# First token block and first weights in halves on two queues, the first weights split in columns, nine warming products

## The chip, the cores and the metric

The kernel runs on one core of one Trainium2 chip. A core has TensorE (PE in the profile, its weight loads PEld), VectorE (DVE), ScalarE (ACT), GpSimd (POOL) and SyncE (SP), and 16 DMA engines that all its queues share. The metric is the device time of one execution in microseconds (us), the median of three runs.

## The reference, cut to what matters

One layer of a hybrid decoder in float32 for 256 prompt tokens and 8 decode tokens, one step each:

```python
x = x + 0.5 * swiglu(rmsnorm(x, n1), f1g, f1u, f1d)      # D_MODEL 2048, D_FF 5504
h = rmsnorm(x, nm)
proj = h @ w_in                                          # q, k, v | RWKV-7 columns
o_att, k_buf, v_buf = attend(q, k, v, sinks)             # window 128, cached K and V for the decode tokens
o_rwkv, shift, S = rwkv_time_mix(proj[..., ATT_COLS:], shift0, wkv0, ...)
x = x + concatenate([o_att, o_rwkv], -1) @ w_out
x = x + 0.5 * swiglu(rmsnorm(x, n2), f2g, f2u, f2d)
```

A final RMSNorm follows, and the new caches and states are outputs too. The time goes into the weight products: 2048 x 5504 matrices, three in each feed-forward part, w_in and w_out.

## The kernel before

The 264 tokens are kept transposed: 16 blocks of 128 features (`KD`) by 264 tokens (`T`). Weights stream from memory in chunks of 128 x 512 float32, 256 KB (`chunk`, L128 to L138): SyncE issues the DMA into `raw` (six buffers), ScalarE casts it to `hi` (L137), and VectorE computes `lo` = raw − hi (`tt`, L64; four buffers of each). The activations are split into high and low parts in the same way. `gemm` (L140 to L155) then makes three matmuls for each 128 x 128 block: hi with the high part, hi with the low part, lo with the high part (all recorded at L80), and adds them up in a bank of PSUM.

`first_ffn` (L302) opens the kernel. `x0` holds the gains of the norm and the first token block, 128 x 280 or 140 KB; ScalarE's queue loads it (L318). `load(0)` splits the block: the high part on ScalarE (L74), the low part on VectorE (L67). The first weight chunk is made ahead of the rest, x1 comes over ScalarE's queue and x2, x3 over SyncE's (L326), the other twelve blocks in groups of four over ScalarE's (L331). Meanwhile TensorE runs `NWARM` products of a tile of ones with itself, which nothing reads.

The mixing stage holds projections, RWKV chunks, attention and w_out at once. Its pieces are generator tasks that are spawned and advanced between weight chunks; the order in which each engine gets its instructions is then set by a list scheduler that simulates the whole program with costs of its own. So an edit at the head can move instructions far behind it. Four things of this stage are spoken of below:

- `m<-kr,bk` on TensorE: products of one RWKV chunk, masked on VectorE into `gm`. SyncE gathers `gm` into `sa` (L520) and loads it back as `X` and `Xt` (L579, L581).
- `dec_scores` (L832): loads the cached keys, `kc`, four times for each half of the heads, 128 KB each, through `load` (L371, ring `ld` of six buffers). Two loads feed the first group of products `m<-qb,ld`, two the second. kc1 to kc4 are those of the second call.
- `dec_attend` (L850): loads `bd`, then `cv`, for the softmax and the values of the decode tokens.
- L946: sixteen reloads of the residual blocks, `x<-xsp`, 132 KB each, over SyncE.

SyncE issues its DMAs strictly in order, so the place in its list decides when a load starts.

Of the kernel before, what the change touches and what calls it, by code (L numbers as in the profile page):

```python
# [7 lines left out]
F32 = mybir.dt.float32  # L8
F32R = mybir.dt.float32r
AF = mybir.ActivationFunctionType  # L10
ALU = mybir.AluOpType
AX = mybir.AxisListType

P = 128
# [10 lines left out]
HALF = (slice(0, 64), slice(64, 128))  # L25
PARTS = [8, 7, 7, 7, 7, 7]
BATCH = [2, 2, 2, 2]
CH, NRAW, NHL = 4, 6, 4
NACC, NM = 3, 5
NH, NQ, NT, NLD = 16, 8, 16, 6  # L30
ROW = 320
NWARM = 11
NGM, NKR, NUV, NTT, NBT = 10, 5, 3, 2, 5
LAG = (11, 7, 7, 7)
P1 = 1
# [17 lines left out]
def body(tc, I, O):  # L53
    nc = tc.nc
    V, A, G, TE, SP = nc.vector, nc.scalar, nc.gpsimd, nc.tensor, nc.sync
# [3 lines left out]
    def uid(s):  # L59
        cnt[0] += 1  # L60
        return f"{s}{cnt[0]}"

    def tt(e, out, a, b, op):
        return e.tensor_tensor(out=out, in0=a, in1=b, op=op)  # L64
# [14 lines left out]
    def mm(out, lhsT, rhs, start=True, stop=True, **k):  # L79
        return TE.matmul(out, lhsT, rhs, start=start, stop=stop, **k)  # L80
# [24 lines left out]
    with ExitStack() as ctx:  # L105
        cp = ctx.enter_context(tc.tile_pool(name="cp", bufs=1))
        sp = ctx.enter_context(tc.tile_pool(name="sp", bufs=1))
        wp = ctx.enter_context(tc.tile_pool(name="wp", bufs=1))
# [8 lines left out]
        def pairs(*rows):  # L117
            return [(t[j], t[j - 1]) for t in rows for j in range(len(t) - 1, 0, -2)]
# [8 lines left out]
        def mp():  # L127
            return pp.tile([P, 512], F32, tag="m", bufs=NM, name=uid("m"))  # L128

        def chunk(src, n, e, ahead=True):  # L130
            w = n * P
            with tc.high_priority() if ahead else nullcontext():
                raw = wp.tile([P, CH * P], F32, tag="raw", bufs=NRAW, name=uid("raw"))
                hi = wp.tile([P, CH * P], F32R, tag="hi", bufs=NHL, name=uid("hi"))
                lo = wp.tile([P, CH * P], F32R, tag="lo", bufs=NHL, name=uid("lo"))
                SP.dma_start(raw[:, :w], src)
                A.copy(hi[:, :w], raw[:, :w])  # L137
                tt(e, lo[:, :w], raw[:, :w], hi[:, :w].bitcast(F32), ALU.subtract)  # L138
            return hi, lo
# [27 lines left out]
        warm = mp()  # L167
        for _ in range(NWARM):
            mm(warm[:, :P], ones, ones)
# [136 lines left out]
        def first_ffn(n2):  # L306
            def load(k0):
                return n1.split(xr[k0], True)

            def nxt(o):  # L310
                n2.split(xr[o])
                n2.square(xr[o])
                A.dma_start(xsp[o], xr[o])

            with tc.tile_pool(name="f1", bufs=1) as fp:
                cur[0] = (fp, NH)
                x0 = fp.tile([P, KD + T], F32, name="x0")
                A.dma_start(x0, I["x0"])  # L318
                n1 = Norm(VG1, pairs(*xs4), ob, gains=x0[:, 0:KD])
                xr = [x0[:, KD:]]  # L320
                at = load(0)
                with tc.issue_after(at.ins):
                    first = chunk(I["gu1"][0, 0][:, 0:CH * P], CH, V, False)
                for e, j0, j1 in ((A, 1, 2), (SP, 2, 4)):
                    xg = fp.tile([P, j1 - j0, T], F32, name=uid("x"))
                    e.dma_start(xg, I["xT"][:, j0:j1, :])  # L326
                    xr += [xg[:, j] for j in range(j1 - j0)]

                def more(q):
                    xg = fp.tile([P, 4, T], F32, tag="x", bufs=3, name=uid("x"))  # L330
                    tc.keep_in_program_order(A.dma_start(xg, I["xT"][:, q * 4:q * 4 + 4, :]))  # L331
                    xr.extend(xg[:, j] for j in range(4))

                ffn(n1, xr, I["gu1"], I["dn1"], nxt, load, more, None, first)
# [703 lines left out]
        kvb, ob, yb = blk("kv", 6), blk("o", 8), blk("y", 8)  # L1038
        n2, n3 = Norm(VGM, pairs(*xs4), ob), Norm(VG2)
        first_ffn(n2)  # L1040
        with tc.tile_pool(name="dx", bufs=1) as dx:
            XD = dx.tile([P, 8, NPAIR, NB], F32, name="XD")
# [103 lines left out]
```

## Time and profile before

| | |
|---|---|
| median of three runs | 1949.77 us (1949.31, 1949.77, 1951.75) |
| profiled execution | 1950.27 us |
| its span | 1948.5 us (1.77 us lie around it) |
| granted TensorE clock, mean | 0.997 |
| TensorE busy | 1934.1 us, 99% of the span |
| DMA, mean | 184 GB/s |

"L80 PE MATMUL acc<-x,hi" in a row is line, engine, operation, and the tiles written and read with their numbers left out. SPq and ACTq rows are DMA issues on SyncE's and ScalarE's queues: a start, and how long the issues of the row took together. A figure in square brackets is the engine's idle time just before, with what ended it. A float32 product of small tiles makes two records of one matmul.

### The profile page before, as it was taken

The page shows a single profiled execution, that of the slowest core. Times are in us where ns is not written, and L with a number is a line of the kernel's source. Part 1 is how long each engine was busy: PE and PEld are TensorE (multiplying, and loading weights), DVE is VectorE, ACT ScalarE, POOL GpSimd, SP SyncE. Part 2 cuts the span into 40 slices and gives each one's busy share as a digit, 9 for nine tenths or more (in the row PEclk, how much of TensorE's full clock was granted, in tenths as well). Part 3 has the DMA queues.
Part 4 walks back from the last instruction along what each step waited for, and adds up shares of the span by engine and source line. Part 5 has one row for each costly group of instructions (what it writes and reads, how often), then busy time and mean ns, then how long its engine had stood idle before and what let it go on. Part 6 is the DMA issues. An engine that isn't in the chain of part 4 may idle for free.

```text
span 1948.5 us, 45522 instructions
## 1 busy us (share of the span) xinstructions
PE 1934.1 (99%) x17131; PEld 1917.4 (98%) x17131; DVE 1307.8 (67%) x2591; ACT 1035.9 (53%) x2069; POOL 260.6 (13%) x382
## 2 busy tenths in 40 slices
PE   9999999999999999999999999999999999999998
PEld 9999999999999999999899999999999999999998
DVE  5865555655556567799867877866666666666665
ACT  5644444444444456666477645644444444444445
POOL 0401102010010112231102100210101001010012
PEclk9999999999999999999999999999999999999999
DMA  7666666665656567565545656566666666666664
GB/s 240 179 194 193 186 194 195 185 189 179 188 182 184 184 193 233 162 173 155 146 133 151 200 157 183 176 187 188 192 191 193 187 193 190 193 194 184 195 181 149
DMA packets 220958, 358.10 MB, mean 184 GB/s; under 512 B 34866, under 2 KB 74434, under 8 KB 220738
## 3 DMA queue, kind: packets, MB, share of 16 engines
q1 hardware_dynamic: 214226, 346.59, 59.6%
q10 hardware_dynamic: 6512, 8.61, 1.3%
q8 instruction: 134, 2.20, 0.4%
q14 instruction: 86, 0.70, 0.1%
HBM read 347.48 MB, written 9.70 MB: 183 GB/s over the span
## 4 chain that ended last, share of the span: by engine, by line
PE 98%; DMA 1%; DVE 1%; ACT 0%; issue 0%; SPq 0%; DVEq 0%; ACTq 0%
PE acc L80 89%; PE m L80 8%; DMA x<-in_x 0%; DMA t<-dr 0%; DVE y L64 0%; DMA ld<-in_cv 0%; PE m L535 0%; DVE lo L64 0%; SPq L581 0%; DMA ld<-in_bias 0%; ACT t L74 0%; PE m L493 0%; PE m L528 0%; PE m L812 0%; ACT hi L137 0%
## 5 line engine op out<-in xcount | busy, mean ns | idle before, releaser
L64 DVE TENSOR_TENSOR lo<-raw,hi 128x512 fp32r<-128x512 f32 (+1 forms) x1288 | 875.6, 683 | 522.8 <-ACT hi L137 499.4
L137 ACT CAST hi<-raw 128x512 fp32r<-128x512 f32 (+1 forms) x1288 | 776.8, 606 | 803.3 <-PE acc L80 724.5
L80 PE MATMUL acc<-x,hi 128*128 128x264 f32 x4840 | 900.2, 287 | 1.5 <-DVE st L64 1.3
L80 PEld LDWEIGHTS acc<-x,hi 128*128 128x128 f32 x4840 | 753.3, 189 | 5.0 <-ACT t L74 1.5
L80 PE MATMUL acc<-x,lo 128*128 128x264 f32 x2420 | 692.8, 286 | 0.0
L80 PE MATMUL acc<-h,hi 128*128 128x264 f32 x2752 | 495.0, 284 | 0.0
L80 PEld LDWEIGHTS acc<-x,lo 128*128 128x128 f32 x2420 | 458.3, 189 | 1.5 <-DVE lo L64 0.4
L80 PEld LDWEIGHTS acc<-h,hi 128*128 128x128 f32 x2752 | 424.4, 189 | 0.0
L80 PE MATMUL acc<-h,lo 128*128 128x264 f32 x1376 | 387.8, 284 | 0.0
L80 PEld LDWEIGHTS acc<-h,lo 128*128 128x128 f32 x1376 | 259.2, 189 | 0.0
L64 POOL TENSOR_TENSOR t<-t,t 128x264 f32<-128x264 f32 x74 | 79.8, 1078 | 1095.6 <-DVE t L64 958.2
L80 PE MATMUL acc<-y,hi 128*128 128x264 f32 x648 | 122.7, 284 | 0.0
L80 PE MATMUL acc<-o,hi 128*128 128x264 f32 x648 | 120.1, 284 | 0.0
L80 PE MATMUL acc<-kv,hi 128*128 128x264 f32 x582 | 109.7, 284 | 0.0
L80 PEld LDWEIGHTS acc<-y,hi 128*128 128x128 f32 x648 | 101.2, 189 | 0.1
L80 PEld LDWEIGHTS acc<-o,hi 128*128 128x128 f32 x648 | 100.1, 189 | 0.0
L67 DVE SCALAR_TENSOR_TENSOR x<-acc,x 128x264 f32<-128x264 f32 x192 | 81.2, 427 | 24.5 <-PE acc L80 23.6
L80 PE MATMUL acc<-y,lo 128*128 128x264 f32 x324 | 92.0, 284 | 0.0
L80 PE MATMUL acc<-o,lo 128*128 128x264 f32 x324 | 92.0, 284 | 0.0
L80 PEld LDWEIGHTS acc<-kv,hi 128*128 128x128 f32 x582 | 90.2, 189 | 0.1
L64 DVE TENSOR_TENSOR t<-acc,t 128x264 f32<-128x264 f32 x156 | 67.4, 432 | 32.8 <-PE acc L80 32.7
L80 PE MATMUL acc<-kv,lo 128*128 128x264 f32 x291 | 82.9, 285 | 0.0
(300 smaller groups left out, 1637.5 us busy)
## 6 DMA issues: line engine op xcount, KB each, us to landing
raw<-in_gu SPq DMA_DIRECT2D x688, 256.0 KB, 3.3
raw<-in_dn SPq DMA_DIRECT2D x224, 256.0 KB, 2.9
raw<-in_win SPq DMA_DIRECT2D x152, 256.0 KB, 3.5
raw<-in_dn SPq DMA_DIRECT2D x160, 192.0 KB, 2.8
raw<-in_wout SPq DMA_DIRECT2D x64, 256.0 KB, 3.5
xsp<-x ACTq DMA_DIRECT2D x16, 132.0 KB, 3.7
x<-xsp SPq DMA_DIRECT2D x16, 132.0 KB, 4.0
ld<-in_sT SPq DMA_DIRECT2D x16, 128.0 KB, 4.4
```

The lines of the kernel that those rows point to most:

```text
L64: return e.tensor_tensor(out=out, in0=a, in1=b, op=op)
L67: return V.scalar_tensor_tensor(out=out, in0=a, scalar=s, in1=b, op0=op0, op1=op1)
L80: return TE.matmul(out, lhsT, rhs, start=start, stop=stop, **k)
L137: A.copy(hi[:, :w], raw[:, :w])
```

## The change

`NWARM` goes from 11 to 9. `x0` and the first weight chunk are each loaded as two halves of 64 partitions, the first 64 by SyncE and the last 64 by ScalarE, x0 first. The DMAs of x1 and of x2, x3 are issued next, and the split of the first block is ordered behind x1's DMA. The cast of the first chunk and its subtraction are each made in two pieces, columns 0 to 127 and 128 to 511, kept in program order behind that split. What is computed stays the same. Lines behind the edit are numbered 10 higher.

```diff
-NWARM = 11
+NWARM = 9
...
-                A.dma_start(x0, I["x0"])
+                raw = wp.tile([P, CH * P], F32, tag="raw", bufs=NRAW, name=uid("raw"))
+                hi, lo = (wp.tile([P, CH * P], F32R, tag=t, bufs=NHL, name=uid(t)) for t in ("hi", "lo"))
+                for d, src in ((x0, I["x0"]), (raw, I["gu1"][0, 0][:, 0:CH * P])):
+                    for e, r in zip((SP, A), HALF):
+                        e.dma_start(d[r], src[r])
                 n1 = Norm(VG1, pairs(*xs4), ob, gains=x0[:, 0:KD])
                 xr = [x0[:, KD:]]
-                at = load(0)
-                with tc.issue_after(at.ins):
-                    first = chunk(I["gu1"][0, 0][:, 0:CH * P], CH, V, False)
                 for e, j0, j1 in ((A, 1, 2), (SP, 2, 4)):
                     xg = fp.tile([P, j1 - j0, T], F32, name=uid("x"))
-                    e.dma_start(xg, I["xT"][:, j0:j1, :])
+                    ins = e.dma_start(xg, I["xT"][:, j0:j1, :])
+                    if e is A:
+                        at = ins
                     xr += [xg[:, j] for j in range(j1 - j0)]
+                with tc.issue_after(at.ins):
+                    at = load(0)
+                with tc.issue_after(at.ins):
+                    for c in (slice(0, P), slice(P, CH * P)):
+                        tc.keep_in_program_order(A.copy(hi[:, c], raw[:, c]))
+                        tc.keep_in_program_order(tt(V, lo[:, c], raw[:, c], hi[:, c].bitcast(F32), ALU.subtract))
+                first = hi, lo
```

The order of the instructions at three places. First ScalarE at the head, before (x_116 is x0, raw_120 the first chunk, x_126 is x1):

```order
L318 DMA x_116<-in_x 128x280
L74 ACT_TABLE_LOAD
L74 ACTIVATE eps<-eps 128x1
L326 DMA x_126<-in_xT 128x264
L74 ACTIVATE x_106<-x_116 128x264
L137 CAST hi_121<-raw_120 128x512
L74 ACTIVATE x_106<-x_126,x_116 128x264
```

and after (x_114 is x0, raw_115 the first chunk, x_122 is x1):

```order
L322 DMA x_114<-in_x 64x280
L74 ACT_TABLE_LOAD
L74 ACTIVATE eps<-eps 128x1
L322 DMA raw_115<-in_gu 64x512
L327 DMA x_122<-in_xT 128x264
L74 ACTIVATE x_104<-x_114 128x264
L335 CAST hi_116<-raw_115 128x128
L335 CAST hi_116<-raw_115 128x384
L74 ACTIVATE x_104<-x_122,x_114 128x264
```

ScalarE's queue has one more DMA, ahead of x1, and the cast is in two pieces; SyncE has the other two halves ahead of x2 and x3.

Second SyncE in the mixing stage, from the third pair of bias loads on, before (ld_16027, ld_16031, ld_16082 and ld_16086 are kc1 to kc4; x_15848 takes the first eight reloads):

```order
L371 DMA ld_15920<-in_bias 128x256
L136 DMA raw_16137<-in_wout 128x512
L371 DMA ld_16027<-in_kc 128x256
L371 DMA ld_16031<-in_kc 128x256
L136 DMA raw_16184<-in_wout 128x512
L136 DMA raw_16213<-in_wout 128x512
L371 DMA ld_16082<-in_kc 128x256
L371 DMA ld_16086<-in_kc 128x256
L946 DMA x_15848<-xsp_90 128x264
```

and after (ld_16084 and ld_16088 are kc3 and kc4; kc1 and kc2 stand first and third behind the bias pair, and left out are kc2, the fourteen reloads ahead of the last two, and two weight chunks):

```order
L381 DMA ld_15922<-in_bias 128x256
L381 DMA ld_16029<-in_kc 128x256
L136 DMA raw_16215<-in_wout 128x512
...
L956 DMA x_15851<-xsp_102 128x264
L956 DMA x_15851<-xsp_103 128x264
L381 DMA ld_16084<-in_kc 128x256
L136 DMA raw_16319<-in_wout 128x512
L381 DMA ld_16088<-in_kc 128x256
L136 DMA raw_16347<-in_wout 128x512
L136 DMA raw_16381<-in_wout 128x512
L381 DMA ld_16168<-in_bd 128x129
```

kc3 and kc4 stood ahead of all sixteen reloads and now stand behind them; the weight chunks stand two places earlier among their own kind.

Third TensorE where it reads them, before (qb_10434 holds the queries of the decode tokens):

```order
L80 MATMUL m_16026<-qb_10434,ld_16031 128x2x4 x2
L80 MATMUL acc_16036<-x_106,hi_16038 128x264 x2
...
L80 MATMUL acc_16036<-x_106,lo_16039 128x264
L812 MATMUL m_16070<-C,t_15546 128x128
...
L814 MATMUL m_16076<-C,t_15547 128x128
L80 MATMUL m_16026<-qb_10434,ld_16082 128x2x4 x2
L80 MATMUL m_16026<-qb_10434,ld_16086 128x2x4 x2
L80 MATMUL acc_16091<-x_106,hi_16093 128x264 x2
```

and after:

```order
L80 MATMUL m_16028<-qb_10436,ld_16033 128x2x4 x2
L80 MATMUL acc_16038<-x_104,hi_16040 128x264
...
L824 MATMUL m_16072<-C,t_15547 128x128
L80 MATMUL m_16028<-qb_10436,ld_16084 128x2x4
L822 MATMUL m_16078<-C,t_15550 128x128
L823 MATMUL m_16078<-C,t_15549 128x128
L824 MATMUL m_16078<-C,t_15549 128x128
L80 MATMUL m_16028<-qb_10436,ld_16084 128x2x4
L80 MATMUL m_16028<-qb_10436,ld_16088 128x2x4 x2
L80 MATMUL acc_16093<-x_104,hi_16095 128x264 x2
```

Counted from the start of TensorE's matmuls with the warming products left out, kc4's first product is number 8979 in both programs, and one product of kc3 has moved ahead of three transposes. The last product `m<-kr,bk` ahead of it is number 8758 before and 8780 after.

## The prediction

> **What bounds the kernel now.** I read the share of each engine first, then the shares of the chain that ended last, then TensorE's waits.
>
> ```profile
> PE 1934.1 (99%) x17131; PEld 1917.4 (98%) x17131; DVE 1307.8 (67%) x2591; ACT 1035.9 (53%) x2069; POOL 260.6 (13%) x382
> PE 98%; DMA 1%; DVE 1%; ACT 0%; issue 0%; SPq 0%; DVEq 0%; ACTq 0%
> ```
>
> TensorE is busy for 99% of the span and holds 98% of the chain. Work on another engine counts only where it makes TensorE wait, or lets its clock fall. The waits that matter here, by what ended them (total, times, longest):
>
> ```profile
> PE m L80 <- issue: 1.7, 1, 1.7
> PE acc L80 <- DVE st L64: 1.3, 1, 1.3
> PE acc L80 <- ACT hi L137: 0.3, 1, 0.3
> PE m L80 <- DMA ld<-in_cv: 0.3, 1, 0.3
> ```
>
> The one wait that the edited code touches is the third, 0.3 us at the head. The others lie in the mixing stage, whose order also moves. The head first: one row of the chain (start, length), the others of the timeline.
>
> ```profile
> 0.73 4.49 DMA x<-in_x
> ```
>
> ```profile
> 0.74 0.40 SPq L136 DMA_DIRECT2D raw<-in_gu  x1
> 0.99 5.06 PE L80 MATMUL m<-ones 128*128 128x128 f32 x22 [0.99 <-POOL eps L164]
> 1.25 0.39 ACTq L326 DMA_DIRECT2D x<-in_xT  x1
> 5.24 0.51 ACT L74 ACTIVATE x<-x 128x264 fp32r<-128x264 f32 x1 [2.56 <-DMA x<-in_x]
> 5.66 0.60 ACT L137 CAST hi<-raw 128x512 fp32r<-128x512 f32 x1
> 6.18 0.51 ACT L74 ACTIVATE x<-x,x 128x264 fp32r<-128x264 f32 x1
> 6.32 0.76 PE L80 MATMUL acc<-x,hi 128*128 128x264 f32 x2 [0.26 <-ACT hi L137]
> 6.91 1.30 DVE L67 SCALAR_TENSOR_TENSOR x<-x,x,x 128x264 fp32r<-128x264 f32 x3
> 7.04 0.39 PE L80 MATMUL acc<-x,lo 128*128 128x264 f32 x1
> ```
>
> The first token block lands at 0.73 + 4.49 = 5.22, ScalarE splits it, casts the first weights, and TensorE starts real work at 6.32. The eleven warming products (two records each, 22) end at 6.05.
>
> **The change: the head.** The DMA share and GB/s are the last two numbers of a window's row; the last row is the time of the first weights from issue to landing.
>
> ```profile
> 4.00:5.00 1.00, 1.00 (x7) 1.00 (x7) 0.00 (x0) 0.00 (x0) 0.00 (x0) 1.00 0.98 344
> 5.00:6.00 1.00, 1.00 (x5) 0.76 (x4) 0.21 (x1) 0.76 (x2) 0.00 (x0) 1.00 1.02 371
> ```
>
> ```profile
> DMA to landing us min/median/max: 4.3/4.3/4.3
> ```
>
> The weights land at 0.74 + 4.3 = 5.05, and the DMA engines are full from 4 us on. Halves move the same bytes. Each queue now issues a half of x0 and then a half of the weights; ScalarE's second issue stood at 1.25 and SP's will stand near 1.2, so the weights are issued 0.45 to 0.5 later. I bound their landing by 4.7 (transfer faster by as much as the issue is later, and a little more) and 5.5 (all of the delay is kept) and take 5.25.
>
> The Trainium skill, page "DMA: Bandwidth & Descriptors", section "Rules for kernel authors", says that two transfers to disjoint partition halves serialize, since both spread over the same 16 engines, and advises one transfer of 128 partitions. It speaks against this part: by it the landing would be the 5.5 end. The full DMA share above agrees with it.
>
> The casts' prices, from the groups by shape (count, busy, mean ns):
>
> ```profile
> L137 ACT CAST hi<-raw 128x512 fp32r<-128x512 f32 x1128 | 697.3, 620 | 727.5 <-PE acc L80 663.4 <-PE m L80 23.1 <-DVE lo L64 8.3
> L137 ACT CAST hi<-raw 128x384 fp32r<-128x384 f32 x160 | 81.9, 512 | 75.8 <-PE acc L80 61.1 <-issue 12.7 <-ACT hi L137 0.5
> L64 DVE TENSOR_TENSOR lo<-raw,hi 128x384 fp32r<-128x384 f32 x160 | 89.5, 559 | 17.6 <-ACT hi L137 17.5
> ```
>
> From 512 to 384 columns a cast loses 0.108 us, so 128 columns cost about 0.30 (estimate). The first cast then ends near 5.25 + 0.30 = 5.55, and TensorE can start near 5.6 in place of 6.32. The nine warming products save two of 0.46 (5.06 / 11) and end near 0.99 + 9 × 0.46 = 5.1; a TensorE idle for 0.5 us is not on the path, since it has no data. But the start is not the gain: the second block needs x1. Its split moves from 6.18 to about 6.0 (splitting the cast adds about 0.1 on ScalarE), its low part on VectorE from 6.91 to about 6.6. TensorE is dense from there on, so the head gives **0.3 us** (from −0.5, the weights at 5.5 with both splits in the way, to +0.55).
>
> **The change: the mixing stage.** No line of it is edited, but its order is: the kept order of SyncE shows the kc loads, which were the second, third, sixth and seventh DMAs after the last bias pair, at places 1, 3, 22 and 24 now, behind all 16 reloads of xsp. TensorE's order shows their second pair of products at the same place. Rows of before, SyncE:
>
> ```profile
> 1063.72 0.56 SPq L579 DMA_DIRECT2D X<-sa  x1
> 1069.92 0.38 SPq L136 DMA_DIRECT2D raw<-in_wout  x1
> 1070.40 0.86 SPq L371 DMA_DIRECT2D ld<-in_kc  x2
> 1072.30 1.15 SPq L371 DMA_DIRECT2D ld<-in_kc  x2
> 1073.54 2.60 SPq L946 DMA_DIRECT2D x<-xsp  x5
> 1082.16 3.79 SPq L946 DMA_DIRECT2D x<-xsp  x4
> ```
>
> Here the landing time of the four kc loads and TensorE's rows of the two groups of products that read them:
>
> ```profile
> DMA to landing us min/median/max: 3.9/4.0/4.1
> ```
>
> ```profile
> 1080.11 0.95 PE L80 MATMUL m<-qb,ld 128*128 128x8 f32 x8
> 1083.13 0.96 PE L80 MATMUL m<-qb,ld 128*128 128x8 f32 x8
> ```
>
> The row at 1069.92 is place 1, that at 1082.16 begins with place 24 (each row's count is added up). If SyncE's issues keep their pace, kc4 goes out at 1082.16 and lands at 1086.2. TensorE wants it in the middle of its second group, 1083.13 + 0.96 / 2 = 1083.6. That is a wait of 2.6 us.
>
> SyncE will be later than that. Its run hangs on X, which waits for the gathers of `gm`, and these on the state products on TensorE:
>
> ```profile
> 1052.95 2.06 PE L80 MATMUL m<-kr,bk 64*128 64x128 f32 x32
> ```
>
> In TensorE's order, warming products left out, the last of these stands 22 matmuls later than before (8780 against 8758), while kc4's first product stands at 8979 in both. The dense rows beside it take 0.12 us for a matmul, so SyncE's run starts 22 × 0.12 = 2.6 us later and kc4 lands at **1088.8**: 1088.8 − 1083.6 = 5.2 us of waiting (about 4.9 of it for kc3 at place 22, the rest for kc4). The 1.3 us wait on `st` lies between the two places, so whether it stays changes nothing here. The later loads of cv gain on TensorE, so the 0.3 us wait goes: **+4.9**. Bounds: +2.3 without the shift; +6.6 with a landing as slow as the slowest reload plus other work before the gathers; 0 or a little below if the loads are issued four or five us sooner than the rows say, for which nothing speaks.
>
> **The clock.** What an idle TensorE does to its clock stands in one place of before (windows: length, then busy time of each engine, then granted clock):
>
> ```profile
> 940.00:942.00 2.00, 0.84 (x42) 0.73 (x38) 0.33 (x2) 0.54 (x3) 0.82 (x5) 1.00 0.98 301
> 942.00:944.00 2.00, 1.50 (x13) 1.43 (x13) 0.00 (x0) 0.92 (x3) 0.00 (x0) 0.54 0.88 221
> 946.00:948.00 2.00, 2.00 (x17) 1.76 (x17) 0.57 (x1) 0.62 (x1) 0.00 (x0) 0.50 0.54 134
> ```
>
> ```profile
> 942.50 0.43 PE L80 MATMUL m<-TT,W 32*32 32x32 f32 x8 [1.66 <-issue]
> 1075.90 0.48 PE L80 MATMUL acc<-x,hi 128*128 128x264 f32 x2 [1.28 <-DVE st L64]
> ```
>
> After 1.66 us without work the clock fell to a half for about 6.5 us; after the 1.28 us at 1075.90 it did not. An idle time of nearly five is far on the side of the first. Half of some 6 dense us is lost: **+3.0** (0 to 3.4).
>
> The Trainium skill, page "TensorE: Matmul & The Clock Gate", section "Part 1: The HAM clock gate", has the clock halved after an idle window of about 3.4 us that runs freely, and restored after a busy one. The 1.66 us above are fewer, so the trace does not bear out that a whole window must be idle; a wait of 4.9 us need not cover a whole free-running window either, and by the strict rule the term could be nothing.
>
> **Sum**, against the profiled execution: 1950.27 − 0.3 + 4.9 + 3.0 = 1957.9. That execution is 0.5 above the median of the three, so against the median it is 1949.77 + 7.6 = **1957.4**.
>
> **The rivals.**
> - The wait for kc comes, the clock holds: 1949.77 − 0.3 + 4.9 = **1954.4** (1951.8 to 1956.1 by the bounds). For it: the products of kc3 and three transposes break the idle time. Against it: 942.50.
> - Only the head changes, because the loads come in time: **1949.5**. It decides at an issue of kc4 by 1079.6, four us ahead of its product. For it: TensorE could be late there by waits that are not in before. Against it: SyncE's pace. If here the halves come late as well, it is 1949.77 + 0.5 = 1950.3: the change then does not do at the head what its words say. By the page on DMA this is the end to expect.
> - Faster: the half-clock stretch at 942.50 goes. It hangs on an idle time of 1.66, and 1.28 did no harm; the phase of whatever sets the clock moves with the head and with the reordering ahead of it. If that idle time falls below 1.28, 3.0 of clock and some 0.4 of waiting come back, and the loads of kc must come in time too: 1949.5 − 3.4 = **1946.1**, with the whole wait gone 1944.9. Against it: TensorE's order still has no gemm between the XD products and this run.
>
> **How the numbers follow.** Chances: wait and half clock 0.42; wait alone 0.25; only the head (either way) 0.22; faster 0.11. This kernel's measurement tells 0.2%, 3.9 us, from no change: above 1953.7 is slower, below 1945.9 faster. Slower: 0.42 and about two thirds of the second, 0.16, together 0.58. Faster: 0.07 of the last case. Same: 0.35. The range takes the bounds of the likeliest (up to 1949.77 − 0.3 + 6.6 + 3.4 = 1959.5) and reaches down over the second case and the third to 1949.0, leaving out the last case and a few hundredths. The forecast's own range is 1954.8 to 1959.5.
>
> **What would show it.** Right: the first real product near 5.6, dense rows 0.3 earlier near 8; a TensorE wait on ld<-in_kc of about 5 us near 1083 to 1089; a granted clock near 0.5 in windows behind it. Wrong: no wait on in_kc (then SyncE's places or TensorE's arrival were misjudged), weights landing after 5.5, a first product held by x1 as long as before, or a half-clock stretch that is missing at 942 or new elsewhere.

## The result, and the profile after

The changed kernel takes 1960.1 us (median of five, 1956.68 to 1960.78) against 1951.09 for the kernel before (median of five runs, 1949.31 to 1951.75). The ratio is 1.0044, 95% interval 1.0033 to 1.0056: about 8.6 us slower. The profiled execution took 1958.66 us, span 1956.8, against 1950.27 and 1948.5. The forecast of 1957.4 stood on 1949.77, the median of three runs; its change of 7.6 us is what compares with the 8.6.

Where along the program do these 8.3 us of span arise? The same subtraction of one weight chunk, early and late, answers that. VectorE's timeline, chunk 520 and chunk 760, of before:

```profile
729.22 0.68 DVE L64 TENSOR_TENSOR lo<-raw,hi 128x512 fp32r<-128x512 f32 x1
1200.04 0.69 DVE L64 TENSOR_TENSOR lo<-raw,hi 128x512 fp32r<-128x512 f32 x1 [0.34 <-ACT hi L137]
```

and the same two chunks after:

```profile
730.86 0.68 DVE L64 TENSOR_TENSOR lo<-raw,hi 128x512 fp32r<-128x512 f32 x1
1208.52 0.69 DVE L64 TENSOR_TENSOR lo<-raw,hi 128x512 fp32r<-128x512 f32 x1 [0.34 <-ACT hi L137]
```

The head is 730.86 − 729.22 = **1.64 us later** where 0.3 earlier was forecast; the mixing stage adds 8.48 − 1.64 = **6.84 us** where 7.9 were forecast (1.63 and 6.85 before rounding, as below). The lag is 1.64 at chunk 20 and 1.63 at chunk 520, 8.48 at chunk 760 and 8.50 at the last chunk, so nothing else adds to it. TensorE's waits after:

```profile
PE m L80 <- issue: 2.9, 1, 2.9
PE m L80 <- DMA ld<-in_kc: 2.5, 1, 2.5
PE m L80 <- ACT BT L550: 1.6, 1, 1.6
PE acc L80 <- ACT hi L335: 1.5, 1, 1.5
PE acc L80 <- DVE st L64: 0.3, 1, 0.3
```

The forecast wait on in_kc is there, at half its size. The head's wait has grown from 0.3 to 1.5, a wait on the copies to `BT` is new, and that on st has shrunk from 1.3.

**The head after**, timeline:

```profile
0.74 0.58 SPq L322 DMA_DIRECT2D x<-in_x  x1
0.99 4.21 PE L80 MATMUL m<-ones 128*128 128x128 f32 x18 [0.99 <-POOL eps L164]
1.44 0.79 ACTq L322 DMA_DIRECT2D raw<-in_gu  x1
3.23 0.52 ACT L74 ACTIVATE x<-x 128x264 fp32r<-128x264 f32 x1 [0.35 <-DMA x<-in_x]
6.35 0.71 ACT L335 CAST hi<-raw 128x128 fp32r<-128x128 f32 x2 [2.61 <-DMA raw<-in_gu]
6.70 0.81 PE L80 MATMUL acc<-x,hi 128*128 128x264 f32 x2 [1.50 <-ACT hi L335]
7.07 0.52 ACT L74 ACTIVATE x<-x,x 128x264 fp32r<-128x264 f32 x1
```

The token block is split at 3.23 in place of 5.24, but the weights are cast at 6.35 in place of 5.66, x1 is split at 7.07 in place of 6.18, and TensorE sat idle for 1.5 us. It then works slowly. Windows from 8 us on (the bracket behind TensorE's busy time counts its matmuls), before:

```profile
8.00:10.00 2.00, 2.00 (x18) 2.00 (x18) 2.00 (x5) 1.72 (x4) 0.00 (x0) 1.00 1.05 418
10.00:12.00 2.00, 2.00 (x19) 2.00 (x18) 0.94 (x3) 0.88 (x2) 0.00 (x0) 1.00 0.98 334
```

and after:

```profile
8.00:10.00 2.00, 2.00 (x9) 1.83 (x9) 1.99 (x5) 1.96 (x4) 0.00 (x0) 1.00 1.05 389
10.00:12.00 2.00, 2.00 (x17) 2.00 (x16) 1.53 (x3) 0.62 (x1) 0.00 (x0) 1.00 0.99 390
```

Nine matmuls in 2 us are half of eighteen: TensorE is still at half speed until about 10 us, though the clock column reads 1.00. The column changes only where a change was recorded; at the start of a program the count of matmuls is the better witness. The first entry of the trace's clock record, at full clock, lies at 6.90 us before and at 10.32 us after.

**The mixing stage after.** SyncE's rows:

```profile
1068.12 0.56 SPq L589 DMA_DIRECT2D X<-sa  x1
1084.15 0.43 SPq L381 DMA_DIRECT2D ld<-in_kc  x1
1086.21 0.43 SPq L381 DMA_DIRECT2D ld<-in_kc  x1
```

TensorE's:

```profile
1085.86 0.27 PE L824 MATMUL m<-C,t 128*128 128x128 f32 x1
1088.61 0.39 PE L80 MATMUL m<-qb,ld 128*128 128x8 f32 x2 [2.47 <-DMA ld<-in_kc]
```

and the windows behind that wait:

```profile
1088.00:1090.00 2.00, 1.39 (x8) 1.33 (x8) 1.69 (x8) 1.98 (x9) 0.00 (x0) 0.73 0.90 284
1090.00:1092.00 2.00, 2.00 (x9) 2.00 (x10) 1.21 (x6) 1.06 (x4) 0.00 (x0) 0.50 0.91 284
1092.00:1094.00 2.00, 2.00 (x11) 2.00 (x11) 0.21 (x1) 0.43 (x1) 0.00 (x0) 0.50 0.81 273
1094.00:1096.00 2.00, 2.00 (x11) 2.00 (x11) 0.96 (x3) 0.19 (x1) 0.00 (x0) 0.56 0.13 47
```

TensorE reaches kc3's product at about 1086.1, waits until 1088.61, and then runs at half clock, from 1088.9 to 1095.8, for 6.8 us. Multiplying the busy time of each window by what its clock lacks gives the loss: 1.39 × 0.27 + 1.0 + 1.0 + 2 × 0.44 = 3.3 us.

### The profile page after: what moved, and what is told of

Same layout as the page of the kernel before. It is cut to its first block, busy times and chain, and to the rows that moved or that the text cites. A ratio compares the mean times of both kernels' runs of the same rounds, so it can differ in the third digit from the quotient of the medians.

```text
span 1956.8 us, 45514 instructions
## 1 busy us (share of the span) xinstructions
PE 1937.1 (99%) x17127; PEld 1920.0 (98%) x17127; DVE 1307.8 (67%) x2592; ACT 1036.4 (53%) x2070; POOL 262.6 (13%) x382
## 4 chain that ended last, share of the span: by engine, by line
PE 97%; DVE 1%; DMA 1%; ACT 0%; issue 0%; SPq 0%; ACTq 0%; POOL 0%; DVEq 0%
PE acc L80 89%; PE m L80 8%; DMA raw<-in_gu 0%; DMA ld<-in_kc 0%; DMA t<-dr 0%; DVE y L64 0%; DVE lo L64 0%; PE m L545 0%; ACT t L74 0%; SPq L956 0%; PE m L503 0%; PE m L822 0%; PE m L538 0%; PE m L823 0%; PE m L824 0%
## 5 line engine op out<-in xcount | busy, mean ns | idle before, releaser
L64 DVE TENSOR_TENSOR lo<-raw,hi 128x512 fp32r<-128x512 f32 (+2 forms) x1289 | 875.7, 683 | 527.1 <-ACT hi L137 502.6
```

## The experiments

The question is split in two: what made the mixing stage longer, and what made the head late. For each run the table has the lag of chunk 520 behind before's profile (the head), what is added up to chunk 760 (the mixing stage), the wait on in_kc, and for the stretch from 820 to 1130 us TensorE's idle time and the loss by half clock, worked out as above from windows of 2 us. "Order" is the order from the mixing stage on.

| run | order | median, us | ratio to before (95%) | head | mixing | in_kc | idle | half clock |
|---|---|---|---|---|---|---|---|---|
| before | old | 1951.09 | 1 | 0 | 0 | none | 4.27 | 3.17 |
| after | new | 1960.1 | 1.0044 (1.0033 to 1.0056) | 1.63 | 6.85 | 2.5 | 8.47 | 4.84 |
| e1_ring8 | new, kc early | 1955.88 | 1.0021 (1.0012 to 1.0030) | 2.94 | 2.73 | none | 6.34 | 3.01 |
| e2_halves_11 | new | 1959.38 | 1.0036 (1.0022 to 1.0050) | 2.49 | 10.55 | 5.0 | 11.14 | 6.16 |
| e3_nine_only | old | 1952.65 | 1.0004 (0.9995 to 1.0013) | 1.26 | 1.56 | none | 4.75 | 4.61 |
| e4_nine_old_order | old | 1952.56 | 1.0001 (0.9991 to 1.0010) | 1.56 | 1.98 | none | 5.43 | 4.25 |
| e5_split_whole_11 | old | 1952.24 | 1.0001 (0.9991 to 1.0011) | 0.65 | 1.62 | none | 5.78 | 3.34 |
| e9_whole_in_series | new | 1961.74 | 1.0046 (1.0033 to 1.0060) | 2.48 | 9.78 | 2.4 | 8.46 | 8.01 |
| e10_old_ring8 | old, bd early | 1953.56 | 1.0005 (0.9996 to 1.0014) | −0.18 | 3.71 | none | 5.33 | 6.08 |

The runs of before that were made beside these had medians of 1951.29 to 1952.28. The profiles of the old order lie 1.6 to 3.7 us above before's in the mixing stage, some mostly by half clock (e3, e10), some by idle time (e5) or both (e4): before's profile was one of the better executions.

**e1: the kc loads ahead of the reloads.**

```diff
-NH, NQ, NT, NLD = 16, 8, 16, 6
+NH, NQ, NT, NLD = 16, 8, 16, 8
```

> The changed kernel with eight buffers in the ring ld in place of six. In the kept order all four kc loads then stand ahead of the sixteen reloads, and TensorE's order differs in 8 matmuls only. Theory 'late loads': the 2.47 us wait on in_kc and the half clock behind it (about 3 us) go, the time falls by 5 to 6 us against the changed kernel, to about 1954, and the head stays 1.6 us late. Rival 'the reordering as a whole': TensorE's order is the cause, the wait turns up on another input (st or the BT copies), and the time falls by less than 2 us.

SyncE's rows of this run show the four kc loads ahead of the sixteen reloads:

```profile
1070.03 0.56 SPq L589 DMA_DIRECT2D X<-sa  x1
...
1074.28 1.49 SPq L381 DMA_DIRECT2D ld<-in_kc  x3
1075.86 0.38 SPq L136 DMA_DIRECT2D raw<-in_wout  x1
1076.34 0.38 SPq L381 DMA_DIRECT2D ld<-in_kc  x1
1076.81 1.33 SPq L956 DMA_DIRECT2D x<-xsp  x3
```

and its windows at the place where the changed kernel fell to half clock:

```profile
1088.00:1090.00 2.00, 2.00 (x20) 2.00 (x19) 1.90 (x12) 1.40 (x7) 0.00 (x0) 1.00 0.72 194
1090.00:1092.00 2.00, 2.00 (x19) 2.00 (x18) 1.69 (x9) 1.98 (x9) 0.00 (x0) 1.00 0.78 232
```

The wait on in_kc and the half clock behind it are gone. The mixing stage costs 2.73 us in place of 6.85, and the ratio falls from 1.0044 to 1.0021, about 4.5 us. That is 'late loads' with a little less than the 5 to 6 us expected. What stays is the new order's 1.6 us on the BT copies, against 1.0 less on st, and a wait of 1.0 at 1112 on copies (`t`, L825) that the changed kernel's profile does not have. The head was 2.9 late here, more than expected: the clock's record begins only at 13.25 us.

**e2: eleven warming products with the halves.**

```diff
-NWARM = 9
+NWARM = 11
```

> The changed kernel with eleven warming products; all behind the head stands in the changed kernel's order. Theory 'late landing': the halves land 1.2 us later whatever is warmed, x1 follows later, and the head stays about 1.6 us late. Rival 'clock': TensorE idles for 1.5 us at nine products and the full clock comes near 10 us in place of 7.2; with eleven it idles for 0.65, the full clock comes by 7 to 8, and the head is only 0.5 to 0.9 us late, so the time falls by about 0.8 to 1 us.

In this profile the weights landed at 6.57 and 6.78, the idle time was 1.7 us and not 0.65, and the clock, which had come up during the warming products, fell to half from about 8.3 to 11.7. The head is 2.49 late: two more products don't bridge the gap. 'Late landing' is the nearer of the two, though it said 1.6; that eleven would save the clock did not hold. The mixing stage has the changed kernel's order and again waits for in_kc, 5.0 us here. This execution took 1963.19 us, the longest of the run's five, so its mixing stage is above the run's usual one.

**e3 and e4: nine products alone.** e3 is the kernel before with this line; e4 also writes the kc loads of a call ahead of its products.

```diff
-NWARM = 11
+NWARM = 9
```

> The kernel before with nine warming products, whole loads, one cast; from the mixing stage on its order is the changed kernel's, word for word. Theory 'late loads': the mixing stage costs its 6.9 us here too, with nothing of the halves in the program: 1957 to 1959. Theory 'clock' for the head: TensorE idles from about 5.2 to 6.3 and the full clock comes later than 7.2; the head is 0.5 to 1.3 us late. Theory 'late landing': the head is within 0.1 us of the kernel before.

> The kernel before with nine warming products and the four kc loads of a call written ahead of its products; from the mixing stage on its order is that of the kernel before, word for word. Beside the run with nine products alone (same head, the other order) it prices the order alone: theory 'late loads' says 6 to 7 us faster than that run and no wait on in_kc; against the kernel before it shows what nine products cost at the head, 0.5 to 1.3 us by 'clock', nothing by 'late landing'. If the two runs agree within 1 us, the cost of the mixing stage comes from the head after all.

The first expectation put the order wrongly: the trace shows the old order in e3 too, kc1 to kc4 ahead of the reloads, so the two are twins and do not price the order, and that they agree within 1 us says nothing on where the mixing stage's cost comes from. They do price the nine products. In both profiles TensorE idles for 1.2 to 1.3 us behind them and the clock falls; windows of e3:

```profile
7.00:8.00 1.00, 1.00 (x7) 0.89 (x7) 0.98 (x4) 1.00 (x3) 0.00 (x0) 0.80 1.07 412
8.00:9.00 1.00, 1.00 (x6) 1.00 (x6) 1.00 (x2) 0.92 (x2) 0.00 (x0) 0.50 1.05 410
9.00:10.00 1.00, 1.00 (x6) 1.00 (x6) 0.91 (x3) 0.62 (x1) 0.00 (x0) 0.50 0.93 371
10.00:11.00 1.00, 1.00 (x7) 1.00 (x7) 0.59 (x1) 0.00 (x0) 0.00 (x0) 0.50 0.97 375
11.00:12.00 1.00, 1.00 (x10) 1.00 (x10) 0.00 (x0) 0.20 (x1) 0.00 (x0) 0.99 0.96 322
```

From about 7.6 to 11.0 it runs at half (8.1 to 11.5 in e4), and the head is 1.26 and 1.56 late, as 'clock' said, e4 a little beyond its 1.3. Over ten runs each the times are the same as before's (1.0004 and 1.0001), so a loss of that size cannot be seen in them.

**e5: the column split alone.** Whole loads, eleven products, old order.

```diff
-                for d, src in ((x0, I["x0"]), (raw, I["gu1"][0, 0][:, 0:CH * P])):
-                    for e, r in zip((SP, A), HALF):
-                        e.dma_start(d[r], src[r])
+                for e, d, src in ((A, x0, I["x0"]), (SP, raw, I["gu1"][0, 0][:, 0:CH * P])):
+                    e.dma_start(d, src)
```

> The column split of the first cast alone: whole loads as in the kernel before, eleven warming products, and from the mixing stage on the order of the kernel before. Theory 'halves and clock': none of the head's loss is left, the weights land near 5.0, the first product starts 0.2 to 0.4 us sooner, the idle time behind the warming products is 0 to 0.2 us and the clock does not fall; the head is 0 to 0.3 us ahead of the kernel before and the time within 1 us of it. Rival 'column split': the two casts delay the split of x1, the head is 0.2 us or more behind.

```profile
5.81 0.70 ACT L334 CAST hi<-raw 128x128 fp32r<-128x128 f32 x2
6.15 0.73 PE L80 MATMUL acc<-x,hi 128*128 128x264 f32 x2
6.92 0.51 ACT L74 ACTIVATE x<-x,x 128x264 fp32r<-128x264 f32 x1 [0.41 <-DMA x<-in_xT]
7.49 0.92 PE L80 MATMUL acc<-x,hi 128*128 128x264 f32 x2 [0.41 <-ACT x L74]
```

TensorE starts 0.17 sooner than before, as the split promises, and then waits for x1, whose landing at 6.9 and not the cast sets the pace. No idle time ahead of the first product, no fall of the clock. The head is 0.65 late by that landing, not 0 to 0.3 early, so the rival's number came true by another cause than the two casts; the time is the same as before's. x1 was issued at 1.25, as in the kernel before, where it was split at 6.18; nothing in the edit moves its issue, and why it landed later in this execution is not known.

**e6 to e8: which halves.** One execution each (1964.94, 1966.90 and 1961.42 us), with eleven products and the split; the mixing stage has other orders there, and of it only the wait on in_kc is read. e6 has x0 in halves and the weights whole, e7 the weights in halves on SyncE's queue alone, e8 the weights in halves on both queues behind a whole x0 (this one as a diff):

```diff
-                for d, src in ((x0, I["x0"]), (raw, I["gu1"][0, 0][:, 0:CH * P])):
-                    for e, r in zip((SP, A), HALF):
-                        e.dma_start(d[r], src[r])
+                A.dma_start(x0, I["x0"])
+                for e, r in zip((SP, A), HALF):
+                    e.dma_start(raw[r], I["gu1"][0, 0][r, 0:CH * P])
```

> Only the token block in halves on two queues, the first weights whole on SyncE's queue behind its half; eleven warming products, column split (the mixing stage has a third order, which is not read here). By 'small pieces wait for issue' (each issue on two queues takes 0.58 us where one took 0.40, and what follows on the queue starts later by that) the weights are issued at 1.35 and land 0.6 us later than now, 5.6 to 5.7. By 'half transfers are slow' (64 partitions move at half the rate) x0 lands soon, as in the changed kernel, and the weights land near 5.1 to 5.4, since they are whole.

> The token block whole on ScalarE's queue, the first weights in two halves of 64 partitions, both on SyncE's queue and ahead of all else there; eleven warming products, column split. By 'half transfers are slow' the second half lands at 6 us or later, as in the changed kernel. By 'small pieces wait for issue' it is issued near 1.2 to 1.3 and lands near 5.3 to 5.6.

> The token block whole on ScalarE's queue, then the first weights in halves of 64 partitions, one first on SyncE's queue, one second on ScalarE's; eleven warming products, column split. By 'half transfers are slow' both halves land at 6 us or later. By 'small pieces wait for issue' the half on SyncE's queue lands by 5.0 and that on ScalarE's by 5.3 to 5.6.

What the DMA queues had moved by 6 us, in the kernel before and in the changed one:

```profile
DMA packets 729, 1.10 MB, mean 184 GB/s; under 512 B 74, under 2 KB 330, under 8 KB 729
```

```profile
DMA packets 536, 0.76 MB, mean 127 GB/s; under 512 B 80, under 2 KB 271, under 8 KB 536
```

and the same of e6 and of e8:

```profile
DMA packets 595, 0.83 MB, mean 139 GB/s; under 512 B 72, under 2 KB 328, under 8 KB 595
```

```profile
DMA packets 691, 1.02 MB, mean 170 GB/s; under 512 B 79, under 2 KB 329, under 8 KB 691
```

e7 had 0.96. In e8 the two halves landed at 4.34 and 5.45, in e7 the cast began at 5.38: weights in halves, with at most one whole x0 ahead of them, are no later than the 5.3 to 5.6 of 'small pieces wait for issue', and 'half transfers are slow' falls for them. But in e6 the whole weights, issued at 1.38, were cast at 6.01, later than either theory allowed. So among these three it is the token block in halves at the front of both queues that delays the weights most: x0 is there 2 us sooner and all else starts behind it. For the head as a whole the three hardly differ, 1.05, 0.82 and 0.81 us late: in e8 TensorE had its weights early and waited for x1, which now stood third on its queue. In none of them did the clock fall at the head.

Their mixing stages cost 10.4 to 15.9 us. In all three at least kc4 stands behind the reloads, and TensorE waits for it or for kc3:

```profile
PE m L80 <- DMA ld<-in_kc: 4.8, 1, 4.8
PE m L80 <- DMA ld<-in_kc: 5.0, 1, 5.0
PE m L80 <- DMA ld<-in_kc: 3.2, 1, 3.2
```

These are e6, e7 and e8 in turn; each wait has 6.8 us of half clock beside it.

**e9: whole loads in series.** x0 and then the weights, both whole, on ScalarE's queue; no halves at all, and the changed kernel's order behind the head.

```diff
-                for d, src in ((x0, I["x0"]), (raw, I["gu1"][0, 0][:, 0:CH * P])):
-                    for e, r in zip((SP, A), HALF):
-                        e.dma_start(d[r], src[r])
+                A.dma_start(x0, I["x0"])
+                A.dma_start(raw, I["gu1"][0, 0][:, 0:CH * P])
```

> No halves: the token block and the first weights are loaded whole, one behind the other on ScalarE's queue, ahead of x1; eleven warming products, column split; from the mixing stage on the order is the changed kernel's, word for word. Head, theory 'in series' (weights that start behind the token block reach their full rate late, whole or in halves): the weights land at 5.7 or later, less than 0.9 MB are moved by 6 us, against 1.10 before, and the head is 0.6 to 2 us late. Rival 'halves': the weights, issued near 1.2, land by 5.4, 1.0 MB or more by 6 us, and the head is at most 0.6 late. Mixing stage, theory 'late loads': a wait on in_kc of 2 to 5 us and a half-clock stretch behind it, the mixing stage 6 to 10 us longer than before. If it is less than 3 us longer, the cost of that order depends on the halves after all.

```profile
DMA packets 730, 1.19 MB, mean 198 GB/s; under 512 B 73, under 2 KB 249, under 8 KB 730
```

```profile
6.29 0.71 ACT L334 CAST hi<-raw 128x128 fp32r<-128x128 f32 x2 [1.39 <-DMA raw<-in_gu]
```

At the head each theory is half right. The weights landed at 6.27, just as in the changed kernel: standing behind x0 is enough to make them late. The head is 2.48 late, beyond both theories, with 1.7 us of it in a fall of the clock from 8.8 to 12.2. The queues lost nothing, 1.19 MB by 6 us: the low rate of 0.72 to 0.83 MB comes with the halves of x0. In the mixing stage 'late loads' holds without a half in the program: 2.4 us on in_kc, a half-clock stretch from 1090.8 to 1097.6, 9.78 us in all (3.2 us more of it by half clock than in the changed kernel's profile), and a ratio of 1.0046, which is the changed kernel's.

**e10: the larger ring in the kernel before.** The edit of e1 in the old order.

> The kernel before with eight buffers in the ring ld: bd and the cv loads can start sooner, the kc loads stand ahead of the reloads as before, and TensorE's order differs in 12 matmuls. Theory 'late loads': nothing is late in the kernel before but cv by 0.3 us, so the gain is 0 to 0.5 us and the time the same. Rival: the larger ring gives a gain of its own, 2 us or more, and then part of what it gave the changed kernel was not the kc loads.

The time is the same (1.0005), so what the ring gave the changed kernel was the earlier kc loads and no merit of its own.

## Why the prediction was wrong

**The step that failed is the head.** It said that the head gives 0.3 us, with 0.5 late as the worst, that the weights land at 5.25 (4.7 to 5.5), and that TensorE's idle time behind nine products "is not on the path, since it has no data". The weights landed at 6.09 and 6.27, x1 was split at 7.07 and not near 6.0, and the head came out 1.6 late. Two things stood outside the bounds. The bounds took the DMA engines as full and shared as before; in fact the issues of halves took 0.58 to 0.79 us and not the 0.40 that was carried over, all that follows on SyncE's queue started a microsecond later (the next weights at 2.62 and not 1.66), and by 6 us a third less was moved. A window of the changed kernel beside the same window of before in the prediction:

```profile
4.00:5.00 1.00, 1.00 (x6) 0.90 (x5) 0.27 (x1) 0.00 (x0) 0.00 (x0) 1.00 0.81 145
```

A DMA share of 0.81 goes here with 145 GB/s, where 0.98 went with 344: the share tells how long transfers were under way and not how much they moved. And the idle time, though nothing could run in it, acted on what ran after it: the clock. The forecast priced an idle TensorE in the mixing stage at 3 us and the same thing at the head at nothing.

In this profile the clock is the larger part. The first real product came 0.38 us later; half of TensorE's busy time from there to the full clock is 1.81 us (6.70 to 10.32), against 0.29 before (6.32 to 6.90). By this estimate the two add up to 1.9, a little more than the 1.63 measured. e3 and e4 point the same way, with heads 1.26 and 1.56 late from nine products alone.

**The mixing stage was right in mechanism, and near in sum**: 6.85 us against 7.9, and e1 and e9 show it from both sides, by taking the loads forward and by keeping the order without the halves. Step by step, with the head's 1.6 us taken off: X goes out at 1066.5, 2.8 us after before's 1063.72 (2.6 forecast); kc4 at 1084.6 (1084.8 forecast). The wait was mis-sized, 2.5 and not 4.9 us, because TensorE came later and the load a little sooner: TensorE reached kc3's product at 1084.5, 1.7 behind what was taken from before, and ran it at 1087.0, where place 22 of before (1081.20) with 2.6 us of shift and 4.0 us to landing gives 1087.8. The sum had noted only what leaves between the two places (st, 1.0 less); it did not see what is new there, 1.6 us on BT and 0.3 on kr, for which before had no row, nor that the wait near 942 would grow by 1.3. All of these lie on TensorE, so the sum changed less than its term. The cv wait went, as forecast.

**The clock** behind kc cost 3.3 us where 3.0 were forecast, after 2.5 us without work. But the stretch near 942 was shorter than before's (1.6 against 3.2 us lost), while its wait grew from 1.7 to 2.9; so the stage's half-clock loss grew by 1.7 only. Idle time grew by 4.2. These add up to 5.9 of the 6.85; the rest I can't place. So the nearness of the sum is in part luck: the wait and the net clock were both smaller than their terms, and waits that were not in the sum and about 1 us without a place filled it up. That the whole change came out near as well, 7.6 against 8.6, is luck again: the head was 1.9 us worse than forecast and the mixing stage 1.0 better.

**The rivals.** Only the head and faster both fell with the wait on in_kc. Halves that come late were foreseen as a rival, at 0.5 us: by the page "DMA: Bandwidth & Descriptors", section "Rules for kernel authors", of the Trainium skill, two halves serialize and one whole transfer is better. The 0.76 MB against 1.10 agree with the advice; its reason explains no loss of rate. Why halves of x0 slow the queues in their first 3 us stays open.

That the clock could hold through the wait for kc (0.25) did not happen in any of the six profiles with that wait (after, e2, e6 to e9). By the strict rule of the Trainium skill, page "TensorE: Matmul & The Clock Gate", section "Part 1: The HAM clock gate", an idle window of about 3.4 us is needed; the clock fell after 2.5, and at the head of e3 after 1.2.

What the times can't show: the runs with the new order and the three forms of the head (after, e2, e9) have ratios of 1.0036 to 1.0046, and those with the old order 1.0001 to 1.0005, though the heads of e3 and e4 are late too. So the order is most of the 8.6 us. How much the head adds is not shown: its 1 to 3 us are read from profiles, which differ from one execution to the next, and no run has the halves of x0 in the old order.

## What to carry to other kernels

An edit at the start of a program whose order a scheduler makes is priced by the order of the whole program, and the place of one load behind sixteen others, 1080 us further on, can outweigh all that was edited. A wait on a saturated TensorE costs its length and then the half clock behind it; a gap that nothing could have filled counts too. Ahead of splitting a load, ask which landing sets the dense stretch: here it was the first weights', with x1's split behind them, and setting them behind x0 made them later.

## What the runs showed of the hardware

- At the head an issue of 64 partitions took 0.57 to 0.60 us (0.79 for the second one on ScalarE's queue in the changed kernel) and one of 128 took 0.38 to 0.42 in the kernel before; two halves cost 1.2 us of a queue. Whole issues right behind halves took 0.54 to 0.78 as well (the changed kernel, e6, e7, e8), so the number of partitions is not all of it.
- The granted clock fell to half for 3.4 us after 1.2 us of idle time at the head (e3), and for 6.8 us after 2.5 us in the mixing stage; 1.28 us at 1075.90 did nothing in the kernel before. In each of the twelve traces the changes of the clock within the span lie whole multiples of 3.41 us apart (to 0.02 us), so half clock comes in pieces of 3.4 us. Of such stretches with 1.4 to 1.7 us of idle time some were followed by half clock (1.45 in e3, 1.52 in e4, 1.49 in e9) and some were not (1.41 in the changed kernel, 1.58 in e1, 1.65 in e7), and in e3, e4, e5 and e10 the clock fell between 1101 and 1104, behind a stretch with no idle time at all in which TensorE ran small products. No threshold follows from these.
- The ten executions of e3 run from 1948.13 us, with a mean granted clock of 0.998, to 1956.45 us, with 0.993.
- The second 132 KB token block landed at 4.8 us in e7 and was first read at 7.3 us in e9; the order of what was issued ahead of it moves it, but not alone: e5 and the kernel before have the same issues and split it at 6.92 and 6.18.
